# Half of the memory tokens turned in strips on VectorE instead of on TensorE

## The chip, the cores and the metric

One core of one Trainium2 chip runs the kernel. The metric is the time of one execution in microseconds of the device. Engines are named as in the profile: PE (TensorE's products), PEld (its weight loads), DVE (VectorE), ACT (ScalarE), POOL (GpSimd) and SP (SyncE, which here only issues DMAs). Each engine takes its instructions in the order of its own list and waits for the others by semaphores.

## The reference

Two layers of an encoder with one mixer each, over 256 tokens `x` of width 2048 and 256 memory tokens `mem` of the same width, all in float32. Cut to what matters here:

```python
for l in range(DEPTH):                      # 2 layers
    h = rmsnorm(x, norm_g[l])
    proj = h @ w_in[l]                      # 2048 x 7168
    ...
    mn = rmsnorm(mem, mem_norm_g[l])
    mkv = mn @ w_mem_kv[l]                  # 2048 x 1024
    mk = rmsnorm(mkv[..., :W_MEM].reshape(b, N_MEM, MEM_HEADS, MEM_HEAD_DIM), mem_k_norm_g[l])
    mv = mkv[..., W_MEM:].reshape(b, N_MEM, MEM_HEADS, MEM_HEAD_DIM)
    ...
    x = x + jnp.concatenate([y_a, y_d, y_m], axis=-1) @ w_out[l]
```

`mkv`, the keys and values of both layers, depends on `mem` alone, and the kernel computes it first: this is the **memory stage**. The sum over the 2048 columns of `mem` is the same in whatever order these are taken, as long as the rows of `w_mem_kv` and the gains of `mem_norm_g` come in that order too.

## The kernel before

A float32 product is made of three in PE's faster format fp32r: each operand is split into a rounded part `hi` and a rest `lo`, and hi·hi, lo·hi and hi·lo are summed in PSUM. ACT makes `hi` (with the gain as a scale, L708 and L253), DVE makes `lo` from the raw value and `hi` (L709 and L254).

The memory stage has 32 steps `g`, 16 for each layer (`k` = g mod 16). Step g takes 128 rows of `w_mem_kv`, 512 KB, which SP loads as `raw` (L700, four buffers; the load of step g+4 waits until `lo` of step g is made), and the 128 x 256 block k of the transposed memory tokens, `memT`, which is made in the first layer and used in both. PE does twelve products of 512 columns in a step: two halves (keys, values) by three products by two blocks of 128 tokens (`products`, L736). At the end of the first layer (steps 14 and 15) only the first half comes in its step, the second halves of both follow together, and steps 16 and 17 begin with their first halves alone; this is the seam of the two layers.

`memT` needs the tokens with columns on the partitions. Before, SP loads them in their natural form into `xs` (`tokens`, L694), PE turns each 128 x 128 block against an identity (`turned`, L714, two transposes a step, called a pair here) into PSUM, and ACT and DVE split it. `xs` is also what ACT sums the squares of `mem` from (`mem_squares`, L654), a quarter at a time.

`x` is turned in another way, beside the memory stage: `x_turned` loads a quarter of it as strips (four DMAs of 32 partitions, rows of 512 B, L611), which DVE turns in 32 x 32 blocks in one instruction of 128 x 1024 (L615); ACT and DVE split the result into `xT` (L256, L257). Turned that way, a quarter of 512 columns comes out dealt by fours: column 4p+j stands on partition p of block j. So `w_in` is loaded in the same order (`x_row_tiles`), and the gains too (`gx`).

The order on the engines of this stage is written by hand: `pin` (and `keep_in_program_order`) holds an instruction at its place in its engine's list. The loop at the end of the stage calls, for step g, the first products, then `operands(g + 2)` (ACT and DVE make the parts of two steps ahead), the other products of the first half, `beside(g)` (all loads, the squares and the start of x's quarters), the second half, and `run_side()`, which takes each side task one part further. Before the loop the first steps are written out: eight products of zeros to warm PE up (`warm`), the transpose `pva` of the 32 x 128 gains `va` into `cva`, the first pair, and the first products in pieces of 256 columns.

## Time and profile before

| what | before |
|---|---|
| median of three runs | 926.02 us (924.58 to 926.31) |
| the profiled execution's own time | 924.49 us |
| its span, first to last instruction | 922.7 us |
| PE busy | 916.9 us, 4176 instructions |
| DVE busy | 669.7 us |
| ACT busy | 494.9 us |
| the memory stage's products end at about | 98 us |

A row of the timeline has the start, the duration, the engine, the line, the operation, the tile written and the tiles read, and xN where N like it are merged (the duration then spans them all); in brackets stands how long the engine was idle before it and what ended that. Matmuls are pipelined, so that the duration of one is longer than the distance to the next; what a step costs PE is read from the starts. A row of waits has the engine, its tile and line, what it waited for, and then the microseconds in total, how often, and the longest. A row of windows has the stretch, its length, for each engine busy time and instructions, then PE's granted clock, the DMA engines' busy share and GB/s.

### The profile page before, as it was taken

What the parts mean: (1) busy time and instruction counts of PE and PEld (TensorE: products, weight loads), DVE (VectorE), ACT (ScalarE), POOL (GpSimd) and SP (SyncE); (2) the same over time, 40 slices, a digit from 0 to 9 for tenths busy, and PEclk for the clock granted to TensorE, in tenths of its full rate; (3) what the DMA queues carried; (4) which work ended last, traced back from release to release, by engine and by line L of the source; (5) the groups of instructions that cost most, each with busy time, mean ns of one, the idle gap of its engine ahead of it and who ended that gap; (6) DMA issues with size and microseconds to landing.
All of it is one profiled execution on the core that took longest, in us unless ns stands there. A gap on an engine that the chain in (4) does not pass through costs nothing.

```text
span 922.7 us, 12256 instructions
## 1 busy us (share of the span) xinstructions
PE 916.9 (99%) x4176; PEld 760.7 (82%) x4176; DVE 669.7 (73%) x1180; ACT 494.9 (54%) x754; POOL 7.0 (1%) x18
## 2 busy tenths in 40 slices
PE   9999999999999999999999999999999999999998
PEld 6888888888888888888888888888888888888886
DVE  5797877857898786557667757878898776558652
ACT  6676645675545554445545544568554554446431
POOL 0001000000000000000000000000000000000000
PEclk9999999999999999999999999999999999999999
DMA  8998878876679999989677867986889989988672
GB/s 265 282 249 310 266 226 234 255 211 196 179 215 249 232 265 247 269 249 244 212 249 249 247 188 225 234 236 177 242 229 228 264 210 259 246 237 241 209 220 74
DMA packets 250226, 215.06 MB, mean 233 GB/s; under 512 B 131166, under 2 KB 176820, under 8 KB 250164
## 3 DMA queue, kind: packets, MB, share of 16 engines
q1 hardware_dynamic: 248004, 210.72, 80.0%
q0 software_dynamic: 672, 2.10, 0.6%
q10 hardware_dynamic: 1488, 1.46, 0.5%
q8 instruction: 33, 0.54, 0.2%
q14 instruction: 29, 0.24, 0.1%
HBM read 193.26 MB, written 20.97 MB: 232 GB/s over the span
## 4 chain that ended last, share of the span: by engine, by line
PE 99%; ACT 0%; DVE 0%; DVEq 0%; issue 0%
PE acc L303 28%; PE acc L302 28%; PE acc L304 28%; PE acc L736 10%; PE po L435 2%; PE s L588 1%; PE s L543 1%; PE s L542 1%; PE warm L123 0%; PE pt L714 0%; ACT hi L708 0%; DVE xs L1003 0%; DVEq L1037 0%; DVE zeros L118 0%; PE pva L804 0%
## 5 line engine op out<-in xcount | busy, mean ns | idle before, releaser
L282 DVE TENSOR_TENSOR lo<-raw,hi 128x1024 fp32r<-128x1024 f32 x288 | 351.9, 1223 | 185.3 <-ACT hi L281 175.8
L281 ACT CAST hi<-raw 128x1024 fp32r<-128x1024 f32 x288 | 302.7, 1052 | 342.0 <-PE acc L304 279.8
L302 PE MATMUL acc<-hi,xT 128*128 128x512 f32 x896 | 350.3, 392 | 0.0
L303 PE MATMUL acc<-lo,xT 128*128 128x512 f32 x896 | 349.0, 390 | 0.0
L304 PE MATMUL acc<-hi,xT 128*128 128x512 f32 x896 | 348.8, 389 | 0.0
L304 PEld LDWEIGHTS acc<-hi,xT 128*128 128x128 f32 x896 | 168.2, 188 | 34.9
L302 PEld LDWEIGHTS acc<-hi,xT 128*128 128x128 f32 x896 | 168.2, 188 | 34.3
L303 PEld LDWEIGHTS acc<-lo,xT 128*128 128x128 f32 x896 | 168.3, 188 | 33.8
L302 PE MATMUL acc<-hi,yT 128*128 128x512 f32 x256 | 99.6, 389 | 0.0
L303 PE MATMUL acc<-lo,yT 128*128 128x512 f32 x256 | 99.6, 389 | 0.0
L304 PE MATMUL acc<-hi,yT 128*128 128x512 f32 x256 | 99.6, 389 | 0.0
L736 PE MATMUL acc<-hi,memT 128*128 128x512 f32 (+1 forms) x260 | 72.2, 392 | 0.6 <-ACT hi L708 0.6
L304 PEld LDWEIGHTS acc<-hi,yT 128*128 128x128 f32 x256 | 48.0, 188 | 10.1
L302 PEld LDWEIGHTS acc<-hi,yT 128*128 128x128 f32 x256 | 48.0, 188 | 10.0
L303 PEld LDWEIGHTS acc<-lo,yT 128*128 128x128 f32 x256 | 48.0, 188 | 9.9
L736 PEld LDWEIGHTS acc<-hi,memT 128*128 128x128 f32 x260 | 47.3, 188 | 10.0 <-ACT hi L708 1.0
L709 DVE SCALAR_TENSOR_TENSOR lo<-raw,cva,hi 128x1024 fp32r<-128x1024 f32 (+2 forms) x37 | 41.5, 1137 | 7.4 <-ACT hi L708 7.0
L708 ACT ACTIVATE hi<-raw,cva 128x1024 fp32r<-128x1024 f32 (+2 forms) x37 | 37.7, 1033 | 11.7 <-DMA raw<-in_w_mem_kv_dram 8.6
L736 PE MATMUL acc<-lo,memT 128*128 128x512 f32 (+1 forms) x130 | 40.1, 390 | 0.0
L736 PEld LDWEIGHTS acc<-lo,memT 128*128 128x128 f32 x130 | 24.2, 188 | 5.2
L553 ACT ACTIVATE e<-e,mx 128x256 f32<-128x256 f32 x48 | 23.8, 499 | 1.4 <-DVE mx L549 1.3
L256 ACT ACTIVATE xT<-xf,gx 128x256 fp32r<-128x256 f32 x32 | 14.4, 499 | 6.8 <-DVE xf L615 6.8
(148 smaller groups left out, 592.5 us busy)
## 6 DMA issues: line engine op xcount, KB each, us to landing
raw<-in_w_in_dram SPq DMA_DIRECT2D x192, 512.0 KB, 4.5
raw<-in_w_out_dram SPq DMA_DIRECT2D x64, 512.0 KB, 4.3
raw<-in_w_in_dram SPq DMA_DIRECT2D x64, 256.0 KB, 4.2
raw<-in_w_mem_kv_dram SPq DMA_DIRECT2D x30, 512.0 KB, 4.5
d<-sh SPq DMA_DIRECT2D x80, 128.0 KB, 4.5
sh<-d SPq DMA_DIRECT2D x64, 128.0 KB, 4.5
d<-yn SPq DMA_DIRECT2D x40, 64.0 KB, 4.2
yn<-d SPq DMA_DIRECT2D x40, 64.0 KB, 4.3
```

The lines of the kernel that those rows point to most:

```text
L256: both = (nc.scalar.activation(hi, src, AF.Copy, scale=gain), nc.vector.scalar_tensor_tensor(lo, src, gain, hi.bitcast(F32), ALU.mult, ALU ...
L281: nc.scalar.copy(hi, raw)
L282: nc.vector.tensor_tensor(lo_, raw, hi.bitcast(F32), ALU.subtract)
L302: nc.tensor.matmul(acc[t], sh, hi, start=first, stop=False)
L303: nc.tensor.matmul(acc[t], sh, lo, start=False, stop=False)
L304: nc.tensor.matmul(acc[t], sl, hi, start=False, stop=last)
L435: nc.tensor.matmul(po[:, t, :], eT[:, i, t, k, :], v[:, k, h * P:(h + 1) * P], start=k == 0, stop=k == NT - 1)
L542: nc.tensor.matmul(s[c][:, i, :], qi, k_first(yT, c, h), start=True, stop=False)
L553: nc.scalar.activation(e[:, c, i], e[:, c, i], AF.Exp, bias=mx[:, c, i:i + 1], accum_out=sm[:, c, i:i + 1])
L708: pin(nc.scalar.activation(hi, raw, AF.Copy, scale=gain))
L709: pin(nc.vector.scalar_tensor_tensor(lo, raw, gain, hi.bitcast(F32), ALU.mult, ALU.subtract))
L736: pin(nc.tensor.matmul(accs[l, half][t][:, at:at + n], memT[:, token_part, k, t * P:(t + 1) * P], p, start=k == 0 and at == 0 and token_pa ...
```

## The change

Memory row tiles 8 to 15 (columns 1024 to 2047 of `mem`) are turned like x: `mem_strips` loads a quarter as strips in steps 2 and 7, `mem_turned` has DVE turn it in steps 5 and 9, and ACT and DVE split the blocks from there instead of from PSUM. The weight rows of k = 8 to 15 are loaded dealt by fours in both layers, and their gains come as `gm_dealt`, two small loads. The natural tokens 8 to 15 are still loaded for the squares, later: in steps 8 and 11 instead of 4 and 8. x's quarters begin in steps 5, 10, 17 and 22 instead of 4, 9, 14 and 19, and the third quarter of the squares in step 12 instead of 11. The constants' small loads begin in step 2 instead of 3.

At the start the warm-up reads a constant of ones that stands in SBUF from the beginning. The gains of steps 0 and 1 come straight from DRAM into `cva_first`, a load of 128 x 2 single elements at the head of ACT's queue; `va` goes behind the first weights there, and its transpose `pva` behind the first products. The transpose `pvb` of the other constants is pinned in step 28.

```diff
+DEALT = 8
...
     def small_loads():
+        for m in range(DEPTH):
+            yield gm_dealt[:, m], mem_norm_g[m, DEALT * P:].rearrange("(q p j) -> p q j", p=P, j=QT)
         yield gx.rearrange("p (m j) -> p m j", j=QT), norm_g.rearrange("l (q p j) -> p (l q) j", p=P, j=QT)
...
-    zeros = tmp.tile([P, NB], mybir.dt.bfloat16, tag="eT", name="zeros")
-    nc.vector.memset(zeros, 0.0)
+    ones = nc.const_aps.tensor(1.0, [P, NB], mybir.dt.bfloat16)
...
-            tc.keep_in_program_order(nc.tensor.matmul(pw, zeros[:, 0:P], zeros, start=True, stop=True))
+            tc.keep_in_program_order(nc.tensor.matmul(pw, ones[:, 0:P], ones, start=True, stop=True))
...
+    cva_first = const.tile([P, 2], F32, name="cva_first")
...
+    gm_dealt = const.tile([P, DEPTH, 2, QT], F32, name="gm_dealt")
     def g_mnorm(l, k):
-        return cva[:, l * KT + k:l * KT + k + 1]
+        if k < DEALT:
+            return cva_first[:, k:k + 1] if l == 0 and k < 2 else cva[:, l * KT + k:l * KT + k + 1]
+        q, j = divmod(k - DEALT, QT)
+        return gm_dealt[:, l, q, j:j + 1]
...
-        nc.tensor.transpose(pb[:, 0:64], vb, ident[0:64, 0:64])
+        pin(nc.tensor.transpose(pb[:, 0:64], vb, ident[0:64, 0:64]))
...
+    def strips_of(src):
         st = tmp.tile([P, SEQ // B, B * QT], F32, tag="e", name=nm("xt"))
         for b in range(NA):
-            tc.keep_in_program_order(nc.sync.dma_start(
+            pin(nc.sync.dma_start(
                 st[b * B:(b + 1) * B], src[:, b * B * QT:(b + 1) * B * QT].rearrange("(n p) r -> p n r", p=B)))
+        return st
+
+    def strips_turned(st):
+        whole = tmp.tile([P, QT, SEQ], F32, tag="sh", name=nm("xf"))
+        pin(nc.vector.transpose(whole.rearrange("p j (n i) -> p j n i", i=B),
+                                st.rearrange("p n (c j) -> p j n c", j=QT)))
+        return whole
...
-        pin(eng.dma_start(raws[g].rearrange("p h c -> p (h c)")[:, at:at + n],
-                          w_mem_kv[l][k * P:(k + 1) * P, at:at + n]))
+        if k < DEALT:
+            rows = w_mem_kv[l][k * P:(k + 1) * P]
+        else:
+            rows = x_row_tiles(w_mem_kv[l], k - k % CK)[:, k % CK]
+        pin(eng.dma_start(raws[g].rearrange("p h c -> p (h c)")[:, at:at + n], rows[:, at:at + n]))
...
+    def mem_strips(q):
+        dealt[q] = strips_of(mem[:, q * NB:(q + 1) * NB])
+
+    def mem_turned(q):
+        dealt[q] = strips_turned(dealt[q])
+
     def token_parts(g):
         if g < KT:
-            split_T(memT, g, turned(g), None, pin=True)
+            split_T(memT, g, turned(g) if g < DEALT else dealt[g // QT][:, g % QT], None, pin=True)
...
         if g + 4 < NG:
-            if g % QT == 0 and g + QT < KT:
-                tokens(g + QT, QT)
+            if g in (0, 8, 11):
+                tokens({0: 4, 8: 8, 11: 12}[g], QT)
             weights(g + 4)
-        if g >= 3:
+        if g in (2, 7):
+            mem_strips(g // 4 + 2)
+        if g in (5, 9):
+            mem_turned(g // 4 + 1)
+        if g >= 2:
             for dst, src in islice(constants, 1):
                 pin(nc.sync.dma_start(dst, src))
-        if g in (4, 9, 14, 19):
-            q = g // 5
+        if g in (5, 10, 17, 22):
+            q = (5, 10, 17, 22).index(g)
...
-        if g in (4, 8, 11, 13):
-            mem_squares((4, 8, 11, 13).index(g))
+        if g in (4, 8, 12, 13):
+            mem_squares((4, 8, 12, 13).index(g))
...
-    pin(nc.scalar.dma_start(va, mem_norm_g.rearrange("l (k p) -> (l k) p", p=P)))
+    pin(nc.scalar.dma_start(cva_first, mem_norm_g[0, 0:2 * P].rearrange("(k p) -> p k", p=P)))
     weights(0, 0, 256, eng=nc.scalar)
     weights(0, NB, NB, eng=nc.scalar)
+    pin(nc.scalar.dma_start(va, mem_norm_g.rearrange("l (k p) -> (l k) p", p=P)))
...
-    pv = ps_t.tile([P, NB], F32, tag="t", name="pva")
-    pin(nc.tensor.transpose(pv[:, 0:32], va, ident[0:32, 0:32]))
-    pin(nc.vector.tensor_copy(cva, pv[:, 0:32]))
     pt = turned(0)
...
             products(0, 0, which, at, 256)
+    pv = ps_t.tile([P, NB], F32, tag="t", name="pva")
+    pin(nc.tensor.transpose(pv[:, 0:32], va, ident[0:32, 0:32]))
+    pin(nc.vector.tensor_copy(cva, pv[:, 0:32]))
```

What the change moves on three engines is shown by their lists, word for word; the numbers at the ends of names tell the tiles apart. First PE in step 6, whose products read hi_286 before and hi_293 now; the pair there is that of block 8. Before:

```order
L736 MATMUL acc_160<-hi_286,memT_106 128x512
L736 MATMUL acc_161<-hi_286,memT_106 128x512
L714 MATMUL pt_339<-ident,xs 128x128 x2
L736 MATMUL acc_160<-hi_286,memT_106 128x512
L736 MATMUL acc_161<-hi_286,memT_106 128x512
```

Now:

```order
L764 MATMUL acc_158<-hi_293,memT_106 128x512
L764 MATMUL acc_159<-hi_293,memT_106 128x512
L764 MATMUL acc_158<-hi_293,memT_106 128x512
L764 MATMUL acc_159<-hi_293,memT_106 128x512
L764 MATMUL acc_158<-lo_294,memT_106 128x512
L764 MATMUL acc_159<-lo_294,memT_106 128x512
```

The pair is gone, and the two blocks' second products follow the first at once; so in steps 6 to 13.

Second DVE, from the rest of step 7's weights (lo_321 before, lo_322 now) to that of step 10's. `xf` is a turned set, `xt` its strips, `xT` x's split. Before:

```order
L709 SCALAR_TENSOR_TENSOR lo_321<-raw_270,cva,hi_320 128x1024
L254 TENSOR_TENSOR memT_106<-pt_339,memT_106 128x256
L709 SCALAR_TENSOR_TENSOR lo_345<-raw_295,cva,hi_344 128x1024
L615 STREAM_TRANSPOSE xf_362<-xt_308 128x1024
L254 TENSOR_TENSOR memT_106<-pt_366,memT_106 128x256
L709 SCALAR_TENSOR_TENSOR lo_372<-raw_328,cva,hi_371 128x1024
L257 SCALAR_TENSOR_TENSOR xT_109<-xf_362,gx,xT_109 128x256 x2
L254 TENSOR_TENSOR memT_106<-pt_394,memT_106 128x256
L709 SCALAR_TENSOR_TENSOR lo_400<-raw_352,cva,hi_399 128x1024
```

Now:

```order
L729 SCALAR_TENSOR_TENSOR lo_322<-raw_277,cva,hi_321 128x1024
L624 STREAM_TRANSPOSE xf_331<-xt_243 128x1024
L262 TENSOR_TENSOR memT_106<-xf_331,memT_106 128x256
L729 SCALAR_TENSOR_TENSOR lo_350<-raw_301,gm_dealt,hi_349 128x1024
L262 TENSOR_TENSOR memT_106<-xf_331,memT_106 128x256
L729 SCALAR_TENSOR_TENSOR lo_372<-raw_329,gm_dealt,hi_371 128x1024
L624 STREAM_TRANSPOSE xf_393<-xt_340 128x1024
L262 TENSOR_TENSOR memT_106<-xf_331,memT_106 128x256
L729 SCALAR_TENSOR_TENSOR lo_400<-raw_357,gm_dealt,hi_399 128x1024
```

The memory's first set (xt_243) is turned between the weights of steps 7 and 8, x's first (xt_340) comes one step later than before; the memory's second set follows behind step 11's weights and x's second behind step 14's.

Third SP's list, the loads from step 6's weights (raw_240 before, raw_241 now) on. Before:

```order
L700 DMA raw_240<-in_w_mem_kv_dram 128x1024
L700 DMA raw_270<-in_w_mem_kv_dram 128x1024
L769 DMA gx<-in_norm_g_dram 128x8x4
L694 DMA xs<-in_mem_dram 128x2x512
L700 DMA raw_295<-in_w_mem_kv_dram 128x1024
L769 DMA vb<-in_conv_w_dram 36x128
L611 DMA xt_308<-in_x_dram 32x8x128 x4
L700 DMA raw_328<-in_w_mem_kv_dram 128x1024
```

Now:

```order
L721 DMA raw_241<-in_w_mem_kv_dram 128x1024
L618 DMA xt_243<-in_mem_dram 32x8x128 x4
L801 DMA gm_dealt<-in_mem_norm_g_dram 128x2x4
L721 DMA raw_277<-in_w_mem_kv_dram 128x1024
L801 DMA gm_dealt<-in_mem_norm_g_dram 128x2x4
L721 DMA raw_301<-in_w_mem_kv_dram 128x1024
L801 DMA gx<-in_norm_g_dram 128x8x4
L721 DMA raw_329<-in_w_mem_kv_dram 128x1024
L801 DMA vb<-in_conv_w_dram 36x128
L618 DMA xt_340<-in_x_dram 32x8x128 x4
```

The first set of strips stands ahead of step 7's weights, where before nothing stood; the natural tokens 8 to 11 have left this part of the list, and the first set of x stands behind step 9's weights instead of step 8's. Further down, the second memory set and tokens 8 to 11 stand together between the weights of steps 11 and 12, and x's second set and tokens 12 to 15 between those of 14 and 15.

More of the change, by code (lines that the diff above doesn't have):

```diff
@@ L604, in mem_out, with x_turned @@
                                            strips(a[:, i, h * P:(h + 1) * P]), ALU.mult, ALU.mult)
-    def x_turned(dst, l, q, src):
+    def strips_of(src):
         st = tmp.tile([P, SEQ // B, B * QT], F32, tag="e", name=nm("xt"))
         for b in range(NA):
-            tc.keep_in_program_order(nc.sync.dma_start(
+            pin(nc.sync.dma_start(
                 st[b * B:(b + 1) * B], src[:, b * B * QT:(b + 1) * B * QT].rearrange("(n p) r -> p n r", p=B)))
+        return st
[4 more added lines that the diff above has]
+        return whole
+    def x_turned(dst, l, q, src):
+        st = strips_of(src)
         yield 2
-        whole = tmp.tile([P, QT, SEQ], F32, tag="sh", name=nm("xf"))
-        tc.keep_in_program_order(nc.vector.transpose(whole.rearrange("p j (n i) -> p j n i", i=B),
-                                                     st.rearrange("p n (c j) -> p j n c", j=QT)))
+        whole = strips_turned(st)
         yield
@@ L715, in turned @@
         return pt
+    dealt = {}
+    def mem_strips(q):
+        dealt[q] = strips_of(mem[:, q * NB:(q + 1) * NB])
+    def mem_turned(q):
+        dealt[q] = strips_turned(dealt[q])
     def token_parts(g):
         if g < KT:
-            split_T(memT, g, turned(g), None, pin=True)
+            split_T(memT, g, turned(g) if g < DEALT else dealt[g // QT][:, g % QT], None, pin=True)
     def operands(g):
```

## Prediction, made before the change was timed

> **What bounds the kernel now.** Read first the page's busy times and chain, then whom PE waited for.
>
> ```profile
> PE 916.9 (99%) x4176; PEld 760.7 (82%) x4176; DVE 669.7 (73%) x1180; ACT 494.9 (54%) x754; POOL 7.0 (1%) x18
> PE 99%; ACT 0%; DVE 0%; DVEq 0%; issue 0%
> PE warm L123 <- DVE zeros L118: 1.2, 1, 1.2
> PE acc L736 <- ACT hi L708: 0.6, 1, 0.6
> ```
>
> PE is busy for 916.9 of 922.7 us, the chain that ends last is PE from end to end, and PE's only two waits in the whole execution (1.2 and 0.6 us) lie in the first 6.3 us. So an instruction taken off PE shortens the kernel, and any new wait of PE lengthens it, one for one. What PE does after step 31 is not touched. The question is the memory stage: what eight pairs of transposes cost on PE there, and whether the engines that feed PE keep up once PE is quicker.
>
> **The pairs that go.** PE's rows in order of time, with a pair in the step and without, and the group of all transposes:
>
> ```profile
> 40.02 0.38 PE L714 MATMUL pt<-ident,xs 128*128 128x128 f32 x2
> ...
> 43.02 0.38 PE L714 MATMUL pt<-ident,xs 128*128 128x128 f32 x2
> ...
> 51.70 1.07 PE L736 MATMUL acc<-hi,memT 128*128 128x512 f32 x4
> ...
> 57.13 1.07 PE L736 MATMUL acc<-hi,memT 128*128 128x512 f32 x4
> L714 PE MATMUL pt<-ident,xs 128*128 128x128 f32 x32 | 6.2, 282 | 0.0
> ```
>
> With a pair, a step of 12 products repeats after 3.00 us. Without one, four halves of six products take 57.13 - 51.70 = 5.43, so a step takes 2.72. A pair is worth 0.27 to 0.28 us (the 282 ns of one transpose overlap its neighbours), and eight of them **2.2 us**. Bounds: 1.1 (only the time from a pair's start to the next product's, about 0.14) and 4.5 (16 x 282 ns); the period is what counts here, so I take 2.2.
>
> **The start.**
>
> ```profile
> 0.87 0.27 DVE L118 MEMSET zeros<- 128x256 uint32 x1 [0.87 <-PEq L1028]
> 1.20 3.60 PE L123 MATMUL warm<-zeros 128*128 128x512 bf16 x8 [1.20 <-DVE zeros L118]
> 4.72 0.31 PE L804 MATMUL pva<-ident,va 32*128 32x32 f32 x1
> 4.96 0.69 PE L714 MATMUL pt<-ident,xs 128*128 128x128 f32 x2
> 5.30 0.91 ACT L708 ACTIVATE hi<-raw,cva 128x256 fp32r<-128x256 f32 x2 [1.37 <-DVE cva L805]
> 6.26 0.95 PE L736 MATMUL acc<-hi,memT 128*128 128x256 f32 x6 [0.61 <-ACT hi L708]
> 6.58 1.34 ACT L708 ACTIVATE hi<-raw,cva 128x512 fp32r<-128x512 f32 x2 [0.37 <-DMA raw<-in_w_mem_kv_dram]
> 7.83 0.62 PE L736 MATMUL acc<-hi,memT 128*128 128x512 f32 x2
> ```
>
> The warm-up waits for a fill of zeros that ends at 1.14; with a constant that is there before, PE can begin at about 0.9: 0.3 saved. The gains' transpose pva no longer stands ahead of the first pair (4.72 to 4.96): 0.24 saved. It is paid again behind the first products, where PE has no gap: net 0.3 at the product of 7.83. That product needs the third hi, ready at 6.58 + 0.67 = 7.25, so at most 0.58 can be won here. The price is unknown in one place: the first hi now waits for cva_first, 256 pieces of four bytes. Its nearest row is va's load in the same place on ACT's queue, which was there for PE at 4.72 at the latest; hi would be wanted from about 4.8. If it came as late as a strip in a full queue (8.1 us, below) the start would lose 4; at an empty queue I take it as hidden, and keep 0 to 0.6 won. **-0.3.** pvb's transpose moves from step 14 to step 28: the same work on a PE that is full in both places, 0; it shortens the way to step 17 by 0.2 us.
>
> **DVE.** What it takes on: two transposes of a strip set (memory rows 8 to 11, 12 to 15), and it keeps the two of x in the same stretch. The rows are the price of one, the stretch from the end of lo(7) to lo(17), and its ends:
>
> ```profile
> L615 DVE STREAM_TRANSPOSE xf<-xt x8: 1991/2014/2037, 30.2 to 524.3; 128x1024 f32<-128x1024 f32 x8
> 25.20:55.40 30.20, 30.20 (x141) 24.31 (x139) 24.68 (x45) 23.98 (x45) 0.00 (x0) 1.00 0.90 267
> 23.94 1.29 DVE L709 SCALAR_TENSOR_TENSOR lo<-raw,cva,hi 128x1024 fp32r<-128x1024 f32 x1 [0.63 <-ACT hi L708]
> 54.11 2.48 DVE L709 SCALAR_TENSOR_TENSOR lo<-raw,cva,hi 128x1024 fp32r<-128x1024 f32 x2
> 56.68 0.62 PE L736 MATMUL acc<-lo,memT 128*128 128x512 f32 x2
> ```
>
> Before, DVE is busy for 24.7 us of the 31.5 from 25.2 to 56.68, when PE wants lo(17) (the first of the two at 54.11). Now it has 24.7 + 2 x 2.0 = 28.7, and PE gets there 2.2 + 0.2 sooner, so it has 29.1. It can't be filled to the last: behind each memory transpose ACT casts the turned tokens and only then makes the next hi (1.15 us), while DVE, in order, waits for that hi; about 1.1 us after the first and 0.4 after the second. 30.2 against 29.1: PE waits **1.0 us** for lo(17), the seam of the two layers, where only half a step's products stand between two weights. Bounds 0 and 2.
>
> **DMA.** Windows (span; busy us and instructions of PE, PEld, DVE, ACT, POOL; clock; DMA share; GB/s), the landing times in the first 50 us, ACT's waits, SP's issues of x's strips and its wait for buffers, and the lead of hi(15):
>
> ```profile
> 10.00:50.00 40.00, 40.00 (x189) 32.22 (x188) 30.50 (x41) 28.72 (x56) 0.00 (x0) 1.00 0.89 271
> 23.20:28.20 5.00, 5.00 (x26) 4.02 (x24) 1.83 (x3) 1.90 (x3) 0.00 (x0) 1.00 1.14 221
> 28.70:36.20 7.50, 7.50 (x36) 6.06 (x35) 7.04 (x9) 5.39 (x13) 0.00 (x0) 1.00 0.91 331
> 36.30:40.30 4.00, 4.00 (x21) 3.21 (x21) 3.51 (x6) 2.85 (x5) 0.00 (x0) 1.00 0.92 239
> xs<-in_mem_dram SPq DMA_DIRECT2D x3, 512.0 KB, 5.5
> xt<-in_x_dram SPq DMA_DIRECT2D x12, 128.0 KB, 8.1
> 27.38 1.15 ACT L708 ACTIVATE hi<-raw,cva 128x1024 fp32r<-128x1024 f32 x1 [1.53 <-DMA raw<-in_w_mem_kv_dram]
> 31.20 1.15 ACT L708 ACTIVATE hi<-raw,cva 128x1024 fp32r<-128x1024 f32 x1 [2.11 <-DMA raw<-in_w_mem_kv_dram]
> 19.96 2.47 SPq L611 DMA_DIRECT2D xt<-in_x_dram  x4
> 34.49 1.81 SPq L611 DMA_DIRECT2D xt<-in_x_dram  x4
> 47.51 2.51 SPq L611 DMA_DIRECT2D xt<-in_x_dram  x4
> SPq L700 <- DVE lo L709: 31.2, 16, 3.7
> 46.70 1.16 ACT L708 ACTIVATE hi<-raw,cva 128x1024 fp32r<-128x1024 f32 x1
> 50.31 1.09 PE L736 MATMUL acc<-hi,memT 128*128 128x512 f32 x4
> ```
>
> The memory's row tiles 8 to 15 are still loaded as they were (their squares need them), so two sets of strips, 0.52 MB each, come on top. x's first set fell into the window at 221 GB/s: 1.10 MB in 5.0 us, of which 0.58 was other work, 1.75 us at the 331 of the window of wide rows; the set cost 3.25 us. The second (239) cost 2.7 in the same way. So two sets are **6.0 us** of DMA (bounds: 3.2 at 331 GB/s, 10 if a set takes its whole window of 5.0; gm_dealt's two small loads lie inside). Against that stand 11% of idle DMA in 10 to 50 us, 4.4; about 1.0 from x's third set, issued at 47.51, which goes three steps later; and the lead of hi(15), ready at 47.86 for a product at 50.31: 2.4. The stretch gets 2.5 shorter. 6.0 + 2.5 - 4.4 - 1.0 - 2.4: the weights of step 15, behind x's second set and tokens 12 to 15 on SP, come **0.7 us** late, and the lo after them with it. SP's queue itself holds little: its weights wait for a buffer 16 times, 31.2 us in all, and the first memory set is issued inside such a wait.
>
> The Trainium skill ("DMA: Bandwidth & Descriptors", Specifications) puts the least transfer for line rate at 512 B, which is a strip's row. The two windows with strips do not show it: 221 and 239 GB/s against 331. By the page a set would cost no more than wide rows, which is rival A.
>
> **The sum.** -2.2 - 0.3 + 1.0 + 0.7 = -0.8 us. On the profiled execution's 924.49 (span 922.7 and 1.8 around it) that is 923.7; the median of the three runs is 926.02, 1.5 above it, so I forecast **925.2**.
>
> **Rivals.** A, the cover holds: strips at the wide rows' price (3.2 instead of 6.0) leave no weight late, and DVE's wait is about half: -2.5 + 0.5 = -2.0, **924.0**. For it: no wait of PE in the stage now, and the first set falls where SP waits for buffers. Against it: DMA share 1.14, and ACT's waits of 1.53 and 2.11 us for weights just behind x's first set.
> B, slower: the strips get the price of x's first set's whole window, 5.0 each, at steps 7 to 15. Then step 15's weights are 4.7 us late, with DVE's 1.0 on top: +3.2, **929.2**. It decides from 3.4 us a set, where the loss eats the gain; the first set's 3.25 is close to that. Against it: the second set, 2.7.
> C, the change doesn't give what its start says: the eight warm-up products take 3.60 us, 0.43 each and twice the later 0.23, and the first pair (0.69 against 0.38) is still slow. Starting sooner may only bring more slow products; a slow stretch of another 3.6 us would lose 1.7: **926.9**. The Trainium skill ("TensorE: Matmul & The Clock Gate", Part 1) has the clock's window run free of the kernel's start, so that its end falls by chance; by that rule this rival can come and go between executions, which no single trace shows.
>
> **How the numbers follow.** Forecast 0.45, A 0.28, B 0.19, C 0.08. The range reaches from A's better half to B's price with a part of the waits spared: 923.5 to 928.8; the forecast's own is 924.2 to 926.4. A measurement can tell 0.2%, 1.85 us, from no change. Faster by more: two thirds of A and the low end of the forecast, 0.27. Slower by more: most of B and a little of C, 0.18. Within it: 0.55.
>
> **What would show it.** Right: PE steps of 2.72 us from step 6, pt rows halved to x16, the first wide product near 7.5, PE waits of about 1 us named lo at step 17 and some tenths named hi or DMA at step 15. A shows no PE wait there; B shows ACT waiting for raw through steps 12 to 16 and PE behind it; C a warm-up whose first wide products are 0.43 apart. Wrong altogether if steps without a pair stay at 3.0 us, or if PE waits behind cva_first at 5 us.

## The result and the profile after

| | before | with the change |
|---|---|---|
| median | 924.45 us (924.19 to 926.31, 6 runs) | 929.04 us (926.9 to 929.9, 6 runs) |
| ratio | 1 | 1.0042, 95% interval 1.0031 to 1.0053 |
| profiled execution, own time | 924.49 | 928.33 |
| span | 922.7 | 926.2 |
| step 3's first product | 15.44 | 16.45 |
| x's first product | 97.94 | 101.58 |

The change made the kernel 0.42% slower. The forecast was 925.2, and its range ended at 928.8. The forecast stood on a median of three runs before, 926.02; all six give 924.45, so that the same -0.8 would have been 923.7. The two profiled executions differ by 3.5 in their spans and by 3.8 in their own times, the medians by 4.6: the changed kernel's profiled execution is one of its shorter ones. What follows explains the 3.5.

The changed kernel's page: busy times, the chain that ended last, and then PE's waits.

```profile
PE 918.2 (99%) x4160; PEld 760.4 (82%) x4160; DVE 673.6 (73%) x1181; ACT 495.7 (54%) x754; POOL 7.0 (1%) x18
PE 94%; DMA 3%; DVE 1%; ACT 1%; issue 0%; SPq 0%; ACTq 0%; DVEq 0%
PE acc L764 <- ACT hi L728: 2.4, 3, 1.4
PE acc L764 <- ACT kraw L773: 0.6, 1, 0.6
PE acc L764 <- DVE lo L729: 0.2, 1, 0.2
```

PE has 16 instructions less, yet it is busy longer (918.2 against 916.9), it waits in four more places, and the chain goes through DMA for the first time. Where the time lies is read from two products that both kernels have, the first of step 3 and the first of x's after the memory stage; first before, then after, from the timeline.

```profile
15.44 0.62 PE L736 MATMUL acc<-hi,memT 128*128 128x512 f32 x2
...
97.94 0.39 PE L302 MATMUL acc<-hi,xT 128*128 128x512 f32 x1
```

```profile
16.45 0.62 PE L764 MATMUL acc<-hi,memT 128*128 128x512 f32 x2
...
25.60 1.07 PE L764 MATMUL acc<-hi,memT 128*128 128x512 f32 x4
26.50 0.61 PE L764 MATMUL acc<-lo,memT 128*128 128x512 f32 x2
...
28.32 1.07 PE L764 MATMUL acc<-hi,memT 128*128 128x512 f32 x4
...
101.58 0.39 PE L310 MATMUL acc<-hi,xT 128*128 128x512 f32 x1
```

The loss has two parts: step 3 begins 1.01 us later, and the **stretch** from there to x's first product takes 85.13 instead of 82.50, 2.63 more. Behind it both kernels need 824.6 to 824.8 us, so nothing is lost or won there. The pairs did go as forecast: step 6 takes 28.32 - 25.60 = 2.72. So the stage's other costs are about 4.8.

They stand at four places. PE's rows at step 12 (42.35), at the first half of step 15 (51.33), and at steps 16 and 17:

```profile
42.35 1.20 PE L764 MATMUL acc<-hi,memT 128*128 128x512 f32 x4 [0.27 <-ACT hi L728]
43.67 0.73 PE L764 MATMUL acc<-lo,memT 128*128 128x512 f32 x2
...
51.33 1.19 PE L764 MATMUL acc<-hi,memT 128*128 128x512 f32 x4 [1.45 <-ACT hi L728]
...
56.70 1.43 PE L764 MATMUL acc<-hi,memT 128*128 128x512 f32 x4 [0.55 <-ACT kraw L773]
...
59.68 0.73 PE L764 MATMUL acc<-lo,memT 128*128 128x512 f32 x2 [0.19 <-DVE lo L729]
```

The brackets show less than is lost, because a matmul's modelled end reaches into the wait. From the starts: a half of a step, 1.36 us without a wait, takes up to 1.9 after a late `hi`, since `lo` is made from `hi` on DVE and comes late too (42.35 to 43.67 for four products, where 25.60 to 26.50 is the usual distance). Counted from start to start over all products, step 12 loses 0.94, step 15 2.12, step 16 (waiting for the keys' copy) 1.08 and step 17 0.46: **4.60**. Minus 2.19 for the pairs, that is 2.41; the other 0.2 of the 2.63 are spread over small gaps.

On ACT the same places show what was late:

```profile
32.84 1.15 ACT L728 ACTIVATE hi<-raw,gm_dealt 128x1024 fp32r<-128x1024 f32 x1 [1.27 <-DMA raw<-in_w_mem_kv_dram]
...
40.63 0.41 ACT L261 CAST memT<-xf 128x256 fp32r<-128x256 f32 x1 [2.46 <-DVE xf L624]
41.15 1.15 ACT L728 ACTIVATE hi<-raw,gm_dealt 128x1024 fp32r<-128x1024 f32 x1
...
50.12 1.15 ACT L728 ACTIVATE hi<-raw,gm_dealt 128x1024 fp32r<-128x1024 f32 x1 [2.40 <-DMA raw<-in_w_mem_kv_dram]
...
52.41 0.89 ACT L264 ACTIVATE xT<-xf,gx 128x256 fp32r<-128x256 f32 x2
53.20 1.14 ACT L728 ACTIVATE hi<-raw,cva 128x1024 fp32r<-128x1024 f32 x1
54.25 0.89 ACT L264 ACTIVATE xT<-xf,gx 128x256 fp32r<-128x256 f32 x2
55.05 1.14 ACT L728 ACTIVATE hi<-raw,cva 128x1024 fp32r<-128x1024 f32 x1
56.09 1.04 ACT L773 COPY kraw<-acc 128x512 f32<-128x512 f32 x2
```

Step 15's `hi` (50.12) waits 2.40 us for its weights to land. Step 12's (41.15) stands behind a cast that waits for DVE's second turn of the memory's strips. The keys' copy (56.09) stands behind the splits of x's second quarter and two steps' `hi`. And the queue of loads, SP's, with the row of DVE that sets the buffer of step 15's weights free (the rest of step 11's weights); first before, where the last row is the load of step 15's weights, then after:

```profile
37.87 1.28 DVE L709 SCALAR_TENSOR_TENSOR lo<-raw,cva,hi 128x1024 fp32r<-128x1024 f32 x1 [0.49 <-ACT hi L708]
39.19 0.35 SPq L700 DMA_DIRECT2D raw<-in_w_mem_kv_dram  x1
```

```profile
37.41 1.29 DVE L729 SCALAR_TENSOR_TENSOR lo<-raw,gm_dealt,hi 128x1024 fp32r<-128x1024 f32 x1 [0.23 <-ACT hi L728]
38.65 2.89 SPq L618 DMA_DIRECT2D xt<-in_x_dram  x4
42.87 0.39 SPq L711 DMA_DIRECT2D xs<-in_mem_dram  x1
43.36 0.41 SPq L721 DMA_DIRECT2D raw<-in_w_mem_kv_dram  x1
```

Before, the load of step 15's weights was issued at 39.19, as soon as its buffer was free. With the change the buffer is free at 38.70, but the load is issued at 43.36, 4.7 us later, behind x's second set and the natural tokens. From there the weights take 6.8 us to land, at 50.12; the median of the weights' loads from 30 to 50 us is 5.6 before and 6.1 with the change. So most of the lateness is what stands ahead of them in SP's list. In part of that time SP itself waits for earlier transfers: from the end of the strips' issue at 41.54 to the tokens at 42.87 it waits for weights to land.

```profile
SPq L711 <- DMA raw<-in_w_mem_kv_dram: 2.2, 2, 1.3
```

The 1.3 us of this row, the longer of its two waits, are that one. The DMA engines in that part of the run, by windows (PE's busy time, its granted clock, the DMA engines' busy share, GB/s), before and then after:

```profile
10.00:50.00 40.00, 40.00 (x189) 1.00 0.89 271
24.00:37.00 13.00, 13.00 (x62) 1.00 0.99 282
```

```profile
10.00:50.00 40.00, 39.48 (x177) 1.00 1.01 274
24.00:37.00 13.00, 13.00 (x59) 1.00 1.08 242
```

The share has gone from 0.89 to 1.01, 4.8 us of engine time, for 3 GB/s x 40 us = 0.12 MB more; from 24 to 37 us the engines are fuller and carry less. By their busy share, no slack is left in this stretch.

The start, last. PE's first rows with the change:

```profile
0.78 3.57 PE L125 MATMUL warm<-const-bfloat16-1.0 128*128 128x512 bf16 x8 [0.78 <-PEq L1061]
4.15 0.63 PE L734 MATMUL pt<-ident,xs 128*128 128x128 f32 x2
5.47 1.65 PE L764 MATMUL acc<-hi,memT 128*128 128x256 f32 x6 [0.69 <-ACT hi L728]
...
8.57 0.92 PE L764 MATMUL acc<-hi,memT 128*128 128x512 f32 x2
```

PE begins 0.42 us earlier and its first product 0.79 earlier, but six products of 256 columns take 1.65 us where they took 0.95. The trace's record of the granted clock has the step from half to full speed at 9.0 us here, and at 5.6 us before. All of the first twelve products ran at half speed. The price that the prediction left open did not fall due: ACT's first `hi`, at 4.91, waited 0.43 us for weights, and not for `cva_first`.

### The profile page after: what moved, and what is told of

The parts are those of the page before. It is cut to its first block, busy times and chain, and to the rows that moved or that the text cites. A ratio compares the mean times of both kernels' runs of the same rounds, so it can differ in the third digit from the quotient of the medians.

```text
span 926.2 us, 12243 instructions
## 1 busy us (share of the span) xinstructions
PE 918.2 (99%) x4160; PEld 760.4 (82%) x4160; DVE 673.6 (73%) x1181; ACT 495.7 (54%) x754; POOL 7.0 (1%) x18
## 4 chain that ended last, share of the span: by engine, by line
PE 94%; DMA 3%; DVE 1%; ACT 1%; issue 0%; SPq 0%; ACTq 0%; DVEq 0%
PE acc L312 28%; PE acc L311 28%; PE acc L310 28%; PE acc L764 6%; PE po L443 2%; DMA raw<-in_w_mem_kv_dram 1%; DMA xt<-in_x_dram 1%; DMA xt<-in_mem_dram 1%; PE s L596 1%; PE s L551 1%; PE s L550 1%; DVE lo L729 0%; ACT hi L728 0%; DVE xf L624 0%; DVE xT L265 0%
## 5 line engine op out<-in xcount | busy, mean ns | idle before, releaser
L729 DVE SCALAR_TENSOR_TENSOR lo<-raw,gm_dealt,hi 128x1024 fp32r<-128x1024 f32 x16 | 20.4, 1283 | 4.2 <-ACT hi L728 4.2
L728 ACT ACTIVATE hi<-raw,gm_dealt 128x1024 fp32r<-128x1024 f32 x16 | 18.2, 1146 | 7.8 <-DMA raw<-in_w_mem_kv_dram 7.2
L624 DVE STREAM_TRANSPOSE xf<-xt 128x1024 f32<-128x1024 f32 x10 | 20.1, 2012 | 1.3 <-DMA xt<-in_x_dram 1.3
```

The source lines that it names most:

```text
L624: pin(nc.vector.transpose(whole.rearrange("p j (n i) -> p j n i", i=B), st.rearrange("p n (c j) -> p j n c", j=QT)))
L728: pin(nc.scalar.activation(hi, raw, AF.Copy, scale=gain))
L729: pin(nc.vector.scalar_tensor_tensor(lo, raw, gain, hi.bitcast(F32), ALU.mult, ALU.subtract))
```

## Experiments

In the table the "stretch" is the one defined above. The expectations call it 82.3 and 84.9, which is 0.23 less: the distance from step 3's second product. Each ratio is to the runs of the kernel before that were made beside that kernel. "Step 3" is when its first product begins, "clock" when the record goes to full speed.

| kernel | median (range, runs) | ratio to before, 95% | step 3 | clock | stretch |
|---|---|---|---|---|---|
| before | 924.45 (924.19 to 926.31, 6) | | 15.44 | 5.6 | 82.50 |
| with the change | 929.04 (926.9 to 929.9, 6) | 1.0031 to 1.0053 | 16.45 | 9.0 | 85.13 |
| the same again | 927.95 (927.31 to 929.21, 5) | 1.0024 to 1.0049 | 17.08 | 9.8 | 85.39 |
| start only | 924.35 (924.09 to 925.94, 11) | 0.9989 to 1.0006 | 15.28 | 4.9 | 82.49 |
| start only, filled | 924.46 (923.94 to 924.71, 11) | 0.9986 to 1.0004 | 14.94 | 4.7 | 82.51 |
| changed, filled | 927.07 (926.08 to 929.15, 9) | 1.0015 to 1.0035 | 15.02 | 4.6 | 85.31 |
| no late tokens | 927.26 (925.15 to 928.74, 11) | 1.0011 to 1.0031 | 17.67 | 3.6, 10.4 | 82.72 |
| x late | 928.45 (922.85 to 929.94, 12) | 1.0011 to 1.0045 | 16.47 | 9.1 | 86.76 |
| weights first | 928.31 (927.27 to 928.74, 5) | 1.0022 to 1.0046 | 16.85 | 10.0 | 85.15 |
| x's last three late | 927.30 (924.55 to 930.89, 12) | 1.0018 to 1.0045 | 16.40 | 9.0 | 82.58 |
| squares from strips | 926.31 (924.59 to 928.37, 12) | 1.0002 to 1.0021 | 16.64 | 9.6 | 85.06 |
| all together | 925.75 (924.06 to 930.77, 11) | 0.9997 to 1.0022 | 14.92 | 5.1 | 84.13 |
| spread | 924.29 (922.53 to 925.93, 11) | 0.9983 to 1.0003 | 16.55 | 9.3 | 81.07 |
| spread, filled | 923.81 (922.52 to 926.86, 11) | 0.9985 to 1.0005 | 14.84 | 3.7 | 81.02 |
| spread, filled, again | 923.97 (923.02 to 926.45, 11) | 0.9978 to 0.9996 | 15.48 | 6.8 | 81.22 |
| x at 7, 10, 17, 20 | 927.01 (925.3 to 929.32, 10) | 1.0011 to 1.0031 | 15.12 | 4.6 | 84.56 |
| x at 10, 15, 18, 21 | 924.24 (922.67 to 927.86, 12) | 0.9981 to 1.0004 | 15.38 | 5.8 | 85.81 |

### The start alone

The kernel before with the parts of the diff that touch the start (the constant `ones`, `cva_first`, `va` and `pva` behind), of which the core is:

```diff
-    zeros = tmp.tile([P, NB], mybir.dt.bfloat16, tag="eT", name="zeros")
-    nc.vector.memset(zeros, 0.0)
+    ones = nc.const_aps.tensor(1.0, [P, NB], mybir.dt.bfloat16)
...
-        return cva[:, l * KT + k:l * KT + k + 1]
+        return cva_first[:, k:k + 1] if l == 0 and k < 2 else cva[:, l * KT + k:l * KT + k + 1]
```

> The kernel before with only the changed start: the warm-up from a constant, the first two gains by their own load, the gains' transpose behind the first products. No strips. Theory W: PE's products double their rate at instants that lie a fixed 3.4 us apart (5.6 us and 9.0 us in the two profiles), and only if PE was kept busy ahead of the instant; the changed start leaves PE idle from 4.8 to 5.5 us, so the faster rate comes at 9.0 instead of 5.6, and step 3 begins near 16.4 instead of 15.44: +1.0 us on the kernel before. Rival R: the instant falls by chance from run to run, and the start has no part in it: medians within 0.3 us of the kernel before, with some runs 1 to 2 us longer in both kernels. Rival S, as the prediction had it: 0.3 us faster.

Its median is 0.1 us under before's, inside the interval: neither the 0.3 won nor the 1.0 lost. The clock went up at 4.9 us, ahead of PE's idle 0.6 us. So theory W as it was written, that the changed start always loses a step of the clock, is wrong. But runs differ: 4 of the 11 lie at 925.37 to 925.94, the others within 924.09 to 924.52. The kernel before shows the same two groups: of the 117 runs of it made beside the experiments, 71 lie at 923.87 to 925.03 and 46 at 925.82 to 926.64, in shares that differ from group to group of runs (8 of 27 to 14 of 28 are long).

### The start, filled

To the changed kernel, and later to "start only", two more warm-up products were added where PE was idle:

```diff
     pt = turned(0)
+    warm(2)
     hi = memT[:, 0, 0, :]
```

> The changed kernel with two more warm-up products behind the first pair, where PE was idle for 0.69 us. Theory W: the faster rate comes near 5.6 us again, the first twelve products of 256 columns take 1.6 us instead of 2.9, and step 3 begins near 15.1 instead of 16.45. What the time makes of it tells whether the seam is set by DMA: if it is (theory D), step 15 still begins near 51.3 us and the total falls by 0.3 at most (928.7 to 929.0); if PE alone sets it, the total falls by 1.3 to 927.7. Rival R (chance): the faster rate comes at 9.0 us or at any instant, nothing changes.

> The kernel before with the changed start and the two more warm-up products, no strips. The stretch is 82.5 as before. The chance of the start alone is seen here: with the idle time filled the runs should lie in one group near 924.1, where the kernel before has a third of its runs at 925.9 to 926.6; if the groups stay as they are, the fill is not what decides.

In the changed kernel step 3 came 1.43 us earlier, as W had it, and the median was lower by 2.0 us than the first group of unfilled runs and by 0.9 than the second; the intervals of the ratios touch. The stretch grew by no more than 0.2, so theory D as put here (step 15 fixed in time whatever the start does) is wrong: the loads begin earlier too when the buffers come free earlier. In the old kernel with the changed start all 11 runs lie in one group, 923.94 to 924.71. If 71 in 117 were the chance of one run, as in the kernel before, 11 in a row would come about once in 240 times. So the idle time ahead of the first product very likely lets a run pay about 1.8 us, and whether it does depends on the instant. That the long runs of these two kernels are those with the later clock is inferred: no long run of either was profiled.

How the clock answers is seen in the run without late tokens, where PE happened to wait 2.34 us at the start for weights. Its windows, with the granted clock ahead of the DMA share:

```profile
3.60:6.90 3.30, 0.96 (x6) 1.00 1.11 380
7.00:10.30 3.30, 3.30 (x14) 0.50 0.93 313
10.40:13.80 3.40, 3.40 (x19) 1.00 0.87 307
```

The clock had risen at 3.56, PE was idle for most of the next stretch, and at 6.97 the clock fell to half, to rise again at 10.38. The changes are 3.41 us apart, one from the next. The Trainium skill ("TensorE: Matmul & The Clock Gate", Part 1) gives a free-running window of 3413 ns; this trace agrees, with 3.41 us between its records. Over the profiles without an idle time ahead of it, the clock rose 2.8 to 6.0 us after PE's start at 0.8 to 1.2, which fits a window whose place is chance. "Start only" is idle there too, and its clock rose at 4.9 us, just as the idle time began. In all eight profiles of kernels with strips and without the fill, which are idle ahead of the first product, it went to full speed for good only at 9.0 us or later; in the seven filled ones it did so at 6.8 us or sooner.

### What makes step 15 wait

Without the natural tokens 8 to 15; the squares of those quarters then read tokens 0 to 7.

```diff
-            if g in (0, 8, 11):
-                tokens({0: 4, 8: 8, 11: 12}[g], QT)
+            if g == 0:
+                tokens(4, QT)
...
-            pin(nc.scalar.activation(sq, xs[:, t, c * NB:(c + 1) * NB], AF.Square, accum_out=ssm[:, t, c:c + 1]))
+            pin(nc.scalar.activation(sq, xs[:, t, c % 2 * NB:(c % 2 + 1) * NB], AF.Square, accum_out=ssm[:, t, c:c + 1]))
```

> The changed kernel without the two loads of natural tokens 8 to 15 (1.05 MB); the squares of these quarters are taken from tokens that are there already, so the row statistics of the memory are other numbers; every instruction of ACT, DVE and PE stays. Theory D (the DMA engines are the bound from 24 to 50 us, and step 15's weights are late because 1.05 MB of strips come on top of natural tokens): step 15's weights come 3 to 4 us earlier, PE's waits at step 15 (2.1 us with the lo behind it), for the keys' copy (1.1) and for lo of step 17 (0.5) go: 929.0 - 3.7 = 925.3. Step 12's wait (1.0) stays if it is DVE's turn that makes it, and goes if DMA makes it (then 924.3). Rival O (the order of work on ACT and DVE makes the waits): all waits stay, 928.5 to 929.5.

And the order of ACT and DVE at blocks 8 to 15:

```diff
     def operands(g):
-        token_parts(g)
-        w_parts(g)
+        if DEALT <= g < KT:
+            w_parts(g)
+            token_parts(g)
+        else:
+            token_parts(g)
+            w_parts(g)
```

> The changed kernel with one exchange: for the blocks that come from strips ACT and DVE make the weights' parts ahead of the token block's parts, so that hi of step 12 doesn't stand on ACT behind a cast that waits for DVE's turn. Measured by the stretch from the first product of step 3 to the first of x's products, which leaves the chance of the start out: 82.3 us before, 84.9 with the change. Theory O (order on ACT): step 12's wait and the lo behind it go, 1.0 us. Theory D (the weights of step 15 come when DMA brings them, whatever PE does ahead): step 15 then waits 1.0 longer, begins at the same distance from step 3 as in the changed kernel (34.8 us), and the stretch stays 84.7 to 85.0. Rival: the stretch falls to 83.9.

Without the loads, step 15's wait was gone. PE's waits in the whole execution; the first line holds the start's 2.34 us and step 12's, and none at step 15:

```profile
PE acc L764 <- ACT hi L728: 2.7, 2, 2.3
PE acc L764 <- ACT kraw L773: 0.3, 1, 0.3
```

The stretch fell from 85.13 to 82.72, by 2.4 of the 3.7 that theory D had. The keys' copy still made PE wait (0.86 with what follows), and so did step 12 (0.99) and step 17 (0.44). The run takes both the 1.05 MB and a place in SP's list ahead of step 15's weights away, so it doesn't tell load and order apart; a kernel that only issues these weights ahead of x's set and the tokens was not run. The profiled execution's own time fell by only 1.1, to 927.26, as its start was 1.2 us later by chance.

With the weights ahead, PE's first two products of step 12 came without a wait, but the next, which needs the rest of the token block, waited in their place (PE's row), and ACT waited for step 12's weights themselves (its row):

```profile
43.51 0.74 PE L768 MATMUL acc<-hi,memT 128*128 128x512 f32 x2 [0.58 <-DVE memT L262]
```

```profile
40.65 1.15 ACT L728 ACTIVATE hi<-raw,gm_dealt 128x1024 fp32r<-128x1024 f32 x1 [2.89 <-DMA raw<-in_w_mem_kv_dram]
```

Step 12 lost 0.85 instead of 0.94, so the exchange moved the wait and hardly made it smaller. The stretch, 85.15, is the one that theory D had, but the run doesn't show that step 15 takes up what is won ahead of it, since nothing was won. The row of step 15:

```profile
51.73 0.73 PE L768 MATMUL acc<-hi,memT 128*128 128x512 f32 x2 [1.58 <-ACT memT L261]
```

The time from step 3 to this product is 34.88 us, as in the changed kernel; as step 12 lost nearly the same, that says little. The changed kernel filled has 35.06. The changed kernel ran again unaltered, for a second profile:

> The changed kernel again, unaltered, for a second profile and more times. If the wait at step 15 is the chain of DMA, it stands in this profile too with 1.3 to 1.9 us, step 15 begins 34.8 to 35.1 us after step 3, and the stretch is 85.1 to 85.4. If the start is chance, step 3 begins at another time than 16.45 us. Median 928 to 929.5.

There the time is 35.17, the wait at step 15 stands again (1.48 from start to start) and the stretch is 85.39, while step 3 began 0.63 us later. Step 12 lost 1.37 there instead of 0.94, and step 15's wait is only 0.13 shorter. So the distance from step 3 to step 15 held within 0.3 us over four profiles, while step 3 itself moved by 2.1.

### x's quarters

The step numbers of x's quarters, first all late and then the last three:

```diff
-        if g in (5, 10, 17, 22):
+        if g in (17, 19, 22, 25):
```

```diff
-        if g in (5, 10, 17, 22):
+        if g in (5, 16, 19, 22):
```

> The changed kernel with x's quarters begun in steps 17, 19, 22 and 25 instead of 5, 10, 17 and 22: two sets of strips (1.05 MB), two turns on DVE (4.0 us) and sixteen split instructions leave the stretch ahead of the seam. Theory D: the weights of step 15 come on time, and step 12's wait goes as DVE is free too; -4.6 us, 924.4. Theory O: DVE's and ACT's order is relieved too, so the same. Rival L: the same work now stands in the second layer, where DVE has 1.3 us of weights and the normed keys in each 2.7 us step: PE waits for lo or hi in steps 18 to 31, as much as is won: 927 to 929.

> The changed kernel with x's second, third and fourth quarter begun in steps 16, 19 and 22 instead of 10, 17 and 22. One set of strips (0.52 MB) leaves the DMA queue ahead of step 15's weights, and the second quarter's turn and splits leave DVE and ACT at steps 13 to 15. Theory X (the second quarter stands on the seam): the waits at step 15 (2.1 with lo), for the keys' copy (1.1) and lo of step 17 (0.5) go, step 12's 1.0 stays: the stretch falls from 84.9 to 81.2 to 81.7. Rival L: the quarters crowd the second layer as in the run with all quarters late, and 1 to 3 us are lost there.

All late, the seam had no wait left at all: steps 12, 15, 16 and 17 ran without one. Rival L came in: the waits moved to the end of the second layer. There, on ACT, a square of x waits for natural tokens, and the last step's `hi` stands behind it; on PE it shows at 97.39:

```profile
94.07 0.63 ACT L660 ACTIVATE sq<-xs 128x512 f32<-128x512 f32 x1 [2.65 <-DMA xs<-in_x_dram]
```

```profile
97.39 1.69 PE L764 MATMUL acc<-hi,memT 128*128 128x512 f32 x4 [2.17 <-ACT hi L728]
```

The wait costs more than itself, for the clock went to half behind it. The window that ends at it, and the one behind:

```profile
94.00:97.80 3.80, 1.63 (x8) 1.00 0.88 307
97.90:101.20 3.30, 3.30 (x9) 0.50 0.44 120
```

At 101.28 it was back at full speed. This kernel has the widest spread of all, 922.85 to 929.94.

With the last three quarters late and the first at its place, step 15, the keys' copy and step 17 had no wait, though the natural tokens were still loaded: step 15's weights were issued 0.35 us after their buffer came free. Step 12 kept its own wait (0.55 in the bracket):

```profile
42.58 1.20 PE L764 MATMUL acc<-hi,memT 128*128 128x512 f32 x4 [0.55 <-ACT hi L728]
```

The stretch is 82.58, not the 81.2 to 81.7 expected, since step 12 cost 1.2 and PE also lost 1.0 near 94 us. It shows what the keys' copy was: the wait went with the second quarter's splits, and stayed in the run without late tokens, which had these splits and no wait at step 15.

### Squares from the strips

The natural tokens 8 to 15 are loaded for their squares alone. In this version ACT sums the squares of the strips, and one small product with `same_p` (ones where two partitions agree mod 32) sums them over the four strips of a token; `same_a` picks each token's own group of partitions:

```diff
+    def strip_squares(q):
+        for n in range(SEQ // B):
+            sq = tmp.tile([P, NB], F32, tag="nat", name=nm("ssq"), bufs=3)
+            pin(nc.scalar.activation(sq[:, 0:P], loose[q][:, n], AF.Square, accum_out=sqs[:, q - 2, n:n + 1]))
+    def strip_sums():
+        sums = ps_t.tile([P, NB], F32, tag="t", name="psq")
+        pin(nc.tensor.matmul(sums[:, 0:16], same_p.rearrange("p a i -> p (a i)"),
+                             sqs.rearrange("p q n -> p (q n)"), start=True, stop=True))
+        for t in range(NT):
+            for q in range(2):
+                pin(nc.vector.tensor_tensor(ssm[:, t, 2 + q * NA:2 + (q + 1) * NA],
+                                            sums[:, q * 8 + t * NA:q * 8 + (t + 1) * NA], same_a, ALU.mult))
...
-            if g in (0, 8, 11):
-                tokens({0: 4, 8: 8, 11: 12}[g], QT)
+            if g == 0:
+                tokens(4, QT)
```

> The changed kernel without the natural tokens 8 to 15, computed in full: ACT sums the squares of the strips themselves (eight pieces of 128 columns a set, in steps 5 and 9), one product of PE sums them over the four strips, and DVE picks them apart. 1.05 MB of loads go, and ACT loses the squares at steps 12 and 13 (2.4 us) at the seam, and does 4.8 us in their place earlier, where it is idle for 3.3 and 2.5 us. Theory D with ACT's order: the waits at step 15, for the keys and of step 17 go (3.7), step 12's stays or grows by 0.5 since ACT's squares stand ahead of its hi: the stretch is 81.2 to 82.0. Rival: ACT's squares make steps 7 to 9 or 12 late by 1 to 2 us, 83.

> The squares from the strips, the weights' parts ahead of the token block's, x's quarters begun in steps 5, 16, 19 and 22, and two more warm-up products, together. If the eight pairs are worth 2.2 us and all of PE's waits in the stage are named, the stretch is 82.3 - 2.2 = 80.1, with up to 0.6 for what is left: 80.1 to 80.7, and the time 922.3 to 923.0, faster than both kernels. If a bound stays that was not named (DMA's share is near 1.0 through most of the stage in both kernels), waits come up at other steps, and the stretch stays over 82.

The first missed its number (85.06 for 81.2 to 82.0): the wait at step 15 was gone, but ACT's eight pieces, 2.4 us a set, stand ahead of `hi`, and step 12 lost 2.4 us in place of 0.94, the steps before it 1.1 and step 17 0.8; its rival had 83. All together also missed (84.13): no wait was left at the seam, but 3.5 us in steps 11 and 12, where the second set landed only at 38 us, behind x's first set. So that set was loaded and turned earlier, x's first quarter loaded later, and the second of the natural squares taken in step 7 instead of 8:

```diff
-        if g in (2, 7):
-            mem_strips(g // 4 + 2)
-        if g in (5, 9):
-            mem_turned(g // 4 + 1)
+        if g in (2, 5):
+            mem_strips(2 + g // 5)
+        if g in (5, 8):
+            mem_turned(2 + g // 8)
...
-        if g in (5, 10, 17, 22):
+        if g in (10, 16, 19, 22):
```

> The version with the squares from the strips, now with the second memory set loaded in step 5 and turned in step 8, x's quarters begun in steps 10, 16, 19 and 22, the weights' parts ahead, and two more warm-up products. The one wait left in the run with everything together (3.4 us in steps 11 and 12) came of the second set, which landed at 38 us behind x's first set and the weights of steps 9 and 10. If that was the cause, the stretch from step 3 to x's first product is 80.1 to 80.8 (82.5 before) and the time 922.4 to 923.2, faster than both. If DMA as a whole is the bound, waits of 1 us or more stay somewhere from step 11 to 17, and the stretch is over 81.5.

> The same without the two more warm-up products. The stretch is the same to 0.2 us. If PE's idle 0.6 us ahead of the first product matters by the instant of the faster rate, a part of the runs is 1 to 3 us longer than the shortest, more of them than with the fill, and the median is 0.3 to 1.5 higher; if it doesn't, the two medians are within 0.3.

The stretch is 81.02 and 81.07: 1.5 us less than before, where 80.1 to 80.8 were expected. The only wait of PE that the view lists for the filled one, but for that ahead of the warm-up (it lies at the start), and its DMA windows:

```profile
PE acc L790 <- ACT hi L750: 0.5, 1, 0.5
```

```profile
10.00:50.00 40.00, 40.00 (x184) 1.00 0.94 269
24.00:37.00 13.00, 13.00 (x59) 1.00 0.93 235
```

PE is without a gap from 10 to 50 us, and the share is back at 0.94. Of the pairs' 2.2, the product for the sums takes 0.15 and a last wait, near 92 to 94 us and too short for that view, 0.36 to 0.41. Between filled and not filled the medians differ by 0.5, with intervals that overlap; here the fill is not shown to matter.

Two more places for x's quarters, to take the last wait away, and the same version again:

> The version with the squares from the strips and two more warm-up products, with x's quarters begun in steps 7, 10, 17 and 20 instead of 10, 16, 19 and 22. Its one wait, 0.25 us for hi at the end of the stage with 0.11 behind it, came of ACT's squares of x, whose natural loads came late. If x's strips in the second layer are what makes them late, that wait goes and the tail of long runs (3 of 11 over 925) with it: the stretch 80.6, median 922.5 to 923.3. If the early stretch has no room for two of x's sets beside the memory's, waits come back at steps 12 to 17 and the stretch is 81.5 or more.

> The same version with x's quarters begun in steps 10, 15, 18 and 21: each of the last three one step earlier. Expected: the wait at the end of the stage goes or falls by half, none comes at the seam, the stretch 80.6 to 80.9. If the turn of the second quarter falls on the seam, the keys' copy or lo of step 17 makes PE wait 0.5 to 1.0: stretch 81.3 to 81.8.

> The version with quarters in steps 10, 16, 19 and 22 and the two more warm-up products again, unaltered, for more times and a second profile: stretch 80.9 to 81.2, PE's faster rate before 5.5 us. If the long runs come of the start, a profile of one shows step 3 near 16.5; if they come of the stage, it shows a wait of PE of 0.5 us or more.

Neither placing is better. With quarters in steps 7 and 10 the seam's waits came back (1.74 and 0.84 us, stretch 84.56): two of x's sets ahead of the seam are too much even without the natural tokens. With 10, 15, 18 and 21 the profiled execution was the longest of its 12 runs, 927.86, while the shortest took 922.67. It shows where this long run comes from. Two of PE's rows and one of ACT's:

```profile
78.59 1.21 PE L790 MATMUL acc<-hi,memT 128*128 128x512 f32 x4 [0.80 <-ACT hi L750]
84.01 0.73 PE L790 MATMUL acc<-lo,memT 128*128 128x512 f32 x2 [1.09 <-DVE lo L751]
```

```profile
94.03 0.63 ACT L660 ACTIVATE sq<-xs 128x512 f32<-128x512 f32 x1 [4.86 <-DMA xs<-in_x_dram]
```

Its start was early (step 3 at 15.38); some 4.5 us are lost from 70 to 98 us, where ACT waits for late loads. The spread and filled version, run twice, is the one that ends under before: medians of 923.81 against 924.47 and 923.97 against 925.42, the second clear of no change (0.9978 to 0.9996), the first not. The second owes much to its neighbours, as 14 of the 28 runs of before in that group are long ones. Over both, the 22 runs have a median of 923.89 and all 117 of before 924.54: about 0.1%, and its longest runs are not shorter than before's. What it gains is the work of several edits together: the strips, the squares from them, the weights' parts ahead, x's quarters moved and the filled start.

## Why the prediction was wrong

The sign was wrong: -0.8 us forecast, +3.5 in the profiled spans. The steps that failed are the lateness of step 15's weights, which the sum put too low because it took SP's queue to hold little, and two waits, the keys' copy and step 12, that the sum didn't have.

**The pairs, -2.2: right.** Steps of 2.72 from step 6, transposes halved to 16. The spread version got 1.5 of it into the time.

**The start, -0.3: not won, and part of the miss is chance.** PE did begin 0.4 us sooner, but in the profiled execution the clock rose 3.4 us later than in the one before, and step 3 came 1.0 us later. That was rival C's mechanism, with a chance of 0.08, and read as a price of more slow products for a start that is sooner. Alone, the changed start cost and won nothing (924.35 against 924.46). The idle 0.6 us lets it happen, as the filled starts show, and it is chance in the kernel before too, since two fifths of its runs are long. That all eight profiles of unfilled kernels with strips show the late clock, and "start only" the early one, is not explained.

**Step 15's weights, +0.7: mis-sized, 2.12.** The weights named were the ones that came late, and runs without late tokens and with x moved took the wait away. But the prediction made their lateness out of the DMA engines' time alone and said that SP's queue holds little. The trace shows the buffer free at 38.70 and the load issued at 43.36, with x's second set, a wait for earlier weights to land and the tokens between; before it was issued 0.03 us after its buffer was free. The load of the DMA engines is in this too, since SP waits for landings. A set of strips was taken at 3.0 us of DMA, and the trace's packets bear that out as an average: those of 512 B took 12.4 us of the 16 engines' time for 2.12 MB from 10 to 50 us, 3.05 a set. Before they took 5.95 us for 1.22 MB, so that the 0.90 MB more cost 6.4 us, or, as an estimate, **3.7 a set**. That is past the 3.4 from which rival B was to decide. And all 4.4 us of idle DMA from 10 to 50 us were set against it, though the windows had less idle where the strips fall: 1% from 24 to 37 us. How much of the 2.12 is SP's order and how much the engines' load stays open.

**lo(17), +1.0: another wait took its place.** At step 17 stand 0.46, but ahead of it 1.08 for the keys' copy, which the sum didn't have. ACT makes that copy in its order, behind the squares and the splits of x's second quarter; the change moved x's quarters by a step, the lateness of the loads by more, and the splits fell on the seam. With that quarter moved away the wait was gone; in the run without late tokens, which had no wait at step 15, it stayed.

**Step 12, not in the sum: 0.94.** Late weights of step 10 (1.27 us) held ACT, then `lo` of step 11, then DVE's second turn behind it, then the cast, then `hi`. This chain is read from the rows; the one run made to break it, with the weights ahead, only moved the wait. Whether a step 12 without a wait would have shortened the kernel, or step 15 would have taken it up, no run shows.

Of the rivals, B gave 929.2, near the 929.04 measured, but as one mechanism; what was measured is late weights worth 2.1 instead of B's 4.7, with C's start and two waits more. That B's number fits is luck.

## What to carry to other kernels

An instruction taken off the bound engine is worth its time only if what feeds the engine has that much room in the same steps. Look at the busy share of the DMA engines in the narrow window where the new loads fall, not over the stage, and price small rows by their own packets: here those of 512 B took 5.8 us per MB, those of 4 KB 2.95. Then follow the queue that issues the loads: compare when a load's buffer comes free with when it is issued, for a load that waits in the list behind others is late however fast it then is. And when an exchange takes a wait away from one product, look at the next products of the same step before calling the wait gone. Here the pairs only paid once the second copy of the tokens was gone and the transfers were spread.

## What the runs showed that was not expected

A wait of PE of 2.2 to 2.3 us cost up to 1.7 us more than itself (an estimate: half of 3.41 us): twice the granted clock went to half right after it (at 97.87 and 6.97 us) for 3.41 us, while no such record follows the wait at step 15 (1.45 in the bracket). The same section of the Trainium skill has the clock fall after at least one idle window of some 3.4 us; here 2.2 us were enough.

The runs of the kernel before lie in two groups, their medians 1.8 us apart, and two products of 0.43 us in an idle place at the start went with 11 of 11 runs in the shorter one. A comparison of a few tenths of a per cent between kernels with different starts has to see many runs, or one fixed stretch of the trace.

A late `hi` costs more than its lateness: the first product after it takes 0.11 us more (0.335 to the next start instead of 0.227). In the trace its own weight load begins with it, both at 42.35, where in a stream without a wait the load begins 0.22 us ahead of its product. And `lo`, made after `hi`, stops PE again four products later.
